# A matrix product by Strassen's scheme on one core: the first product of six regions in quarters, its sums on VectorE, kept sums of b for two more column pairs, and output stored in pairs of row tiles

## The chip, the core and the metric

The kernel runs on one core of a Trainium2 chip. A core has five engines that run side by side and meet through semaphores: TensorE (matmuls; called PE in the profile, its weight loads PEld), VectorE (DVE), ScalarE (ACT), GpSimd (POOL) and SyncE (SP). TensorE writes to PSUM, which has 8 banks of 512 float32 columns by 128 partitions; the other data lie in SBUF, and DMA queues move them from and to DRAM. A queue belongs to the engine that issues into it. Here SP issues plain copies, ScalarE a few, and POOL the loads that round float32 to float16 on the way. Every engine runs its instructions in the order in which the program lists them.

The metric is device time in microseconds (us) of one execution, the median of several.

## What is computed

```
a, b: 4096 x 4096, float32, normally distributed;  alpha = 0.01
x = a @ b
out = where(x > 0, x, alpha * x)
```

## The kernel before

**Regions.** The output is cut into 4 groups g of 1024 rows and 4 pairs j of two 512-column tiles. One (g, j) is a region of 1024 x 1024 results, four blocks of 512 x 512. Region (0, 0) is made plainly at the start. The other 15 follow in the order of a list: (0, 1) to (0, 3); then (1, 2), (1, 0), (1, 3), (1, 1); (2, 2), (2, 0), (2, 3), (2, 1); and (3, 2), (3, 0), (3, 1), (3, 3). The last region of groups 0 to 2 is called turning: the next group's rows of a are brought in and transposed there.

**Seven products.** Each region is a 2 x 2 block product, with the inner dimension of 4096 cut in two halves of 2048, by Winograd's form of Strassen's scheme: seven products of 512 x 2048 by 2048 x 512 in place of eight. A half of the inner dimension consists of two tiles k of 1024 rows. The products are numbered from 0: a11·B11, a12·B21, s2·T2, s3·T3, s1·T5, a22·T4 and s4·B22, where s1 to s4 are sums of blocks of a, made once for a group, and the T are sums of blocks of b, made by VectorE for every region, in place, by `b_sum` (L603) on tiles of 128 x 4096: T3 = B22 - B12 in B12's tile, T2 = B11 + T3 in B11's, T4 = B21 - T2 in B21's, T5 = B22 - T2 in B11's tile again. The order in a region is product 0, then T3 and T2, product 1, T4, product 2, T5, product 4, product 3, product 5, product 6. The program's names call the last four fifth, fourth, sixth and seventh.

**Plain and in quarters.** A plain product (`product`, L831) has 64 matmuls of 512 columns: 2 tiles k, 8 chunks of 128 rows, 4 row tiles mt, each mt with a bank of its own. A product in quarters applies the scheme once more to one product: seven quarter products (`quarter_product`, L770) of 16 matmuls with 256 columns, each with sums of quarters of its operands, of 2048 elements a partition (`sums_of_b` L702 to L706, `t3_of_b` L696). Quarter sums of a's operands s1, a22 and s4 are made once for a group (`sums_of_a`, L719, in the group's second region for s1) and stored in DRAM; later regions load them (`load_sums`, L762). Quarter sums of s3 are made by `sums_of_s3` (L753). In groups 1 to 3, in the regions that are neither the first of their group nor turning, products 4, 3, 5 and 6 are in quarters; 0, 1 and 2 are plain. The set `FIFTH` names the regions with product 4 in quarters: they are just those seven.

**Banks.** Four banks hold y, four hold z. Product 0 goes to y; ScalarE copies y to z (L1132); product 1 adds to z, which is copied out (`keep`, L844) as block u1; product 2 adds to y, and so on. y and z change places from region to region. The leaky step (`leaky`, L313) runs on VectorE, and `leave` stores a block: one DMA of 256 KB for every row tile of 128 rows, on SP (L1076).

**Rooms.** Three rooms of a pool called a16 hold quarter sums, squares and loaded pieces in turn: a new tile waits for the last use of the one whose room it takes. A larger pool x holds the s tiles and a tile q of four quarter sums. s2 is loaded anew for every region, one half k by `load_s2` at the end of the region before, the other during T3: a small memset on VectorE (L788) stands ahead of that load (L789).

**Loads of b.** `fetch_b` and `fetch_unit` load the next region's blocks as soon as a tile is free: from b by POOL with rounding (L547), or, where a float16 copy was kept in DRAM, by SP (L542, L544). For the pair j = 2 (`CACHED`) the sums T3 and T2 are kept too, by group 1, and groups 2 and 3 load them (`move_t`, L529): T3 in place of B12, T2 on ScalarE's queue once product 0 has read B11.

**Measures.** The kernel judges whether its inputs are regular enough for this scheme: `Measure` squares four pieces of a block on ScalarE (L231; three in `begin`, one in `end`) and folds them on VectorE (L240 to L264). `EARLY` and `MEASURED` name the blocks that a region measures. The first entry of `EARLY` begins ahead of product 0 and ends behind it; a second one begins after the copies to z and ends after T2; the entry `middle` (B22 in (3, 0) and (3, 3)) likewise.

## Time and profile before

| what | value |
|---|---|
| median of 3 runs | 1524.78 us (1524.66 to 1526.13) |
| the profiled execution's own time | 1526.13 us |
| its span, first to last instruction | 1524.2 us |
| granted TensorE clock | 0.999 of full speed |
| regions (1, 0), (1, 3) | 91.85 and 91.90 us |
| regions (2, 0), (2, 3), (3, 0), (3, 1) | 90.34, 90.35, 90.34 and 90.35 us |
| DMA traffic | 372.29 MB, 244 GB/s on average |

A row of a timeline gives the start in us from the span's start, the length, the engine, the line of the kernel, the operation, the tile written and those read, shapes, and how many equal instructions were merged. In square brackets is the engine's idle time before it and what ended that. A matmul's length overlaps with the next one's start, so rates are read from start to start. "DMA to landing" is the time from issue to the last byte. The chain of waits is followed back from the last instruction: at each step to what released it.

### The profile page before, as it was taken

How to read it: one execution, taken by the hardware profiler on the slowest of the kernel's cores; microseconds unless marked ns; L12 is line 12 of the kernel's file. 1: busy time of each engine (PE TensorE's matmuls, PEld its weight loads, DVE VectorE, ACT ScalarE, POOL GpSimd, SP SyncE). 2: the span in 40 equal slices, each digit the busy share in tenths (PEclk: the TensorE clock that was granted, in tenths of full speed). 3: DMA queues.
4: the chain of work that ended last, by engine and by line, in shares of the span. 5: the costliest groups of instructions: out<-in, count | busy, mean ns of one | idle time of the engine just before them, and what ended most of it. 6: DMA issues, size and time to landing. Idle time of an engine off the chain costs nothing.

```text
span 1524.2 us, 22803 instructions
## 1 busy us (share of the span) xinstructions
PE 1512.9 (99%) x9003; PEld 879.2 (58%) x9003; DVE 1166.7 (77%) x1221; ACT 512.2 (34%) x885; POOL 258.3 (17%) x426
## 2 busy tenths in 40 slices
PE   9999999999999999999999999999999999999998
PEld 4444444444446577584544748667554475848667
DVE  4588867666896597777779598777978779888797
ACT  2411535537410123124661132323574113252221
POOL 5641110233202011012320101000331100101000
PEclk9999999999999999999999999999999999999999
DMA  9999995999889999999898968859999894968935
GB/s 247 189 215 206 242 285 164 174 187 193 235 330 247 285 300 288 290 289 271 199 273 317 287 252 187 312 151 330 220 239 313 223 337 148 276 238 205 331 122 172
DMA packets 197767, 372.29 MB, mean 244 GB/s; under 512 B 19345, under 2 KB 132241, under 8 KB 184594
## 3 DMA queue, kind: packets, MB, share of 16 engines
q0 software_dynamic: 119808, 112.22, 46.7%
q1 hardware_dynamic: 71218, 232.95, 41.0%
q10 hardware_dynamic: 6624, 25.56, 4.3%
q8 instruction: 72, 1.18, 0.3%
q14 instruction: 45, 0.37, 0.1%
HBM read 359.66 MB, written 121.11 MB: 315 GB/s over the span
## 4 chain that ended last, share of the span: by engine, by line
PE 58%; DMA 6%; DVE 1%; issue 1%; SPq 0%; POOL 0%; DVEq 0%; POOLq 0%
PE ps L831 34%; PE ps L770 25%; DMA b<-in_b_dram 5%; DMA q<-kept_qs 1%; DVE b L603 0%; DVE c L313 0%; DVE c L1028 0%; POOL b L547 0%; SPq L1076 0%; DVE b L696 0%; DVE b L1225 0%; SPq L762 0%; DVEq L603 0%; DVEq L313 0%; POOLq L547 0%
## 5 line engine op out<-in xcount | busy, mean ns | idle before, releaser
L831 PE MATMUL ps<-b,a 128*128 128x512 f16 x2624 | 570.6, 379 | 0.0
L831 PEld LDWEIGHTS <-a 128*128 128x128 f16 x2624 | 256.7, 98 | 307.8
L831 PE MATMUL ps<-b,s 128*128 128x512 f16 x1792 | 391.3, 379 | 0.0
L831 PEld LDWEIGHTS <-s 128*128 128x128 f16 x1792 | 175.4, 98 | 210.9
L603 DVE TENSOR_TENSOR b<-b 128x4096 f16<-128x4096 f16 x97 | 218.9, 2286 | 51.3 <-DMA b<-in_b_dram 33.1
L547 POOL DMA_DIRECT2D b<-in_b_dram x128 | 94.8, 745 | 870.5 <-PE ps L770 266.1
L770 PEld LDWEIGHTS <-q 128*128 128x128 f16 x1872 | 182.6, 98 | 23.2 <-DMA q<-kept_qs 1.6
L844 ACT COPY c<-ps 128x512 f32<-128x512 f32 x164 | 85.9, 596 | 287.5 <-PE ps L831 277.7
L133 POOL DMA_DIRECT2D a<-in_a_dram x252 | 137.5, 553 | 246.5 <-ACT junk L622 81.3
L142 DVE STREAM_TRANSPOSE a<-a 128x512 uint32<-128x512 uint32 (+2 forms) x120 | 127.0, 1107 | 66.5 <-DMA a<-in_a_dram 66.5
L313 DVE SCALAR_TENSOR_TENSOR c<-c 128x1024 f32<-128x1024 f32 (+2 forms) x123 | 141.9, 1196 | 17.7 <-ACT c L844 17.4
L622 ACT ACTIVATE junk<-a 128x512 bf16<-128x512 f16 x192 | 121.2, 631 | 72.8 <-DMA a<-in_a_dram 67.7
L770 PEld LDWEIGHTS <-a 128*128 128x128 f16 x1200 | 117.4, 98 | 14.7
L231 ACT ACTIVATE sq<-b 128x2048 bf16<-128x2048 f16 x60 | 111.3, 1911 | 43.1 <-DVE sq L240 36.7
L770 PE MATMUL ps<-b,q 128*128 128x256 f16 x1008 | 118.6, 273 | 0.0
L283 PE MATMUL ps<-b,a 128*128 128x512 f16 x512 | 112.2, 379 | 0.5 <-ACT a L380 0.2
L770 PEld LDWEIGHTS <-s 128*128 128x128 f16 x960 | 93.8, 98 | 14.2 <-DVE b L603 1.3
L770 PE MATMUL ps<-q,q 128*128 128x256 f16 x864 | 99.9, 273 | 0.9 <-DMA q<-kept_qs 0.9
L770 PE MATMUL ps<-b,a 128*128 128x256 f16 x752 | 88.3, 273 | 0.0
L283 PEld LDWEIGHTS <-a 128*128 128x128 f16 x512 | 49.7, 98 | 60.8 <-issue 1.4
L1132 ACT COPY ps<-ps 128x512 f32<-128x512 f32 x60 | 32.8, 572 | 147.8 <-PE ps L831 147.8
L1063 DVE TENSOR_TENSOR c<-ps,c 128x512 f32<-128x512 f32 x72 | 44.6, 683 | 47.6 <-PE ps L831 38.0
(125 smaller groups left out, 1053.6 us busy)
## 6 DMA issues: line engine op xcount, KB each, us to landing
b<-in_b_dram POOLq DMA_DIRECT2D x136, 512.0 KB, 12.4
out_dram<-c SPq DMA_DIRECT2D x240, 256.0 KB, 7.8
a<-in_a_dram POOLq DMA_DIRECT2D x244, 128.0 KB, 5.7
b<-kept_half SPq DMA_DIRECT2D x28, 1024.0 KB, 11.8
b<-kept SPq DMA_DIRECT2D x20, 1024.0 KB, 9.2
q<-kept_qs ACTq DMA_DIRECT2D x40, 512.0 KB, 7.2
s<-kept_s SPq DMA_DIRECT2D x18, 1024.0 KB, 9.1
q<-kept_qs SPq DMA_DIRECT2D x28, 512.0 KB, 6.1
```

Source lines behind the costliest of these rows:

```text
L133: nc.gpsimd.dma_start(a16[32 * q:32 * q + 32], src.rearrange("(g i) w -> i g w", i=32))
L142: nc.vector.transpose(part.rearrange("p c m e -> p c (m e)").bitcast(U32) .rearrange("p c (g i) -> p g c i", i=32), src[:, :, i * n:(i + 1 ...
L231: nc.scalar.activation(to, self.parts[n], SQUARE)
L283: nc.tensor.matmul(ps, a_cols(at[0, h, u], c, mt, (h, u) == (0, 0)), bt[0, u, nt][:, c, :], start=first, stop=last,)
L313: nc.vector.scalar_tensor_tensor(t, t, alpha, t, op0=MULT, op1=MAX if alpha <= 1 else MIN)
L547: nc.gpsimd.dma_start(t[:, c:c + 4, :], b_rows(j, u, c, 4, nt, g > 0))
L603: nc.vector.tensor_tensor(f(to), f(x0), f(x1), op)
L622: nc.scalar.activation(junk, piece[:, q, :], SQUARE, accum_out=to[:, 4 * n + q:4 * n + q + 1])
L770: nc.tensor.matmul(to[m], xq[:, c // 2, rows, c % 2], yq[:, c, :], start=first and c == 0 and m < banks, stop=c == KC - 1, skip_group_chec ...
L831: nc.tensor.matmul(banks[mt], a_cols(t, c, mt, t is first_a), B(half, nt, k)[:, c, :], start=first and (k, c) == todo[0], stop=(k, c) == t ...
L844: nc.scalar.copy(kept[mt], banks[mt])
L1063: nc.vector.tensor_add(to, bank, to)
```

## The change

Line numbers of the changed kernel are 6 to 117 higher than before for the same statement.

1. A set `FIRST` of six regions replaces `FIFTH`: (1, 0), (1, 3), (2, 3), (3, 0), (3, 1) and (3, 3). The region (2, 0) is not in it. In these product 0 is in quarters (`first_in_quarters`). The sums of quarters of a11 and of B11 are made by VectorE (`for_the_first`), in pieces between the quarter products of the seventh product of the region before, into rooms that that product gives free. The last sum of b is made inside product 0.
2. In these six regions a bank holds a quarter of a block (two row tiles by 256 columns) rather than a row tile of 512 columns, so products 1 and 2 have 128 matmuls of 256 columns each. Adds and copies go by quarters. The banks are dealt out anew: y and z rotate so that product 0 finds free banks, and its first copy goes to the bank that the seventh product called "other".
3. In these regions all entries of `EARLY` begin after product 0's copies and end after T2, and the first half of s2 is loaded after product 0. `EARLY` itself is dealt out differently: (2, 0) has none, (1, 1) measures B11, (3, 0) measures B21, (3, 1) only B21.
4. T3 and T2 of the pairs 0 and 3 are stored in group 2 and loaded in group 3. Where T2 is loaded, a measure begins and ends at once, and the memset and load of s2's second half come behind it.
5. `leave` stores two row tiles by one DMA of 512 KB.

```diff
+KEPT_T = {CACHED: 1, 0: 2, 3: 2}
...
+    def places(g, h, mt, j, nt):
+        row = ((g * 2 + h) * MT + mt) * P
+        col = (j * 2 + nt) * NT
+        return out[row:row + 2 * P, col:col + NT].rearrange("(m p) n -> p m n", p=P)
...
-        if g > 1 and j == CACHED and (half, nt) == (0, 1):
-            move_t("t3", t, u, False)
+        if g > KEPT_T.get(j, G) and (half, nt) == (0, 1):
+            move_t("t3", j, t, u, False)
...
-        (1, 3): [B11], (2, 0): [B21], (2, 3): [B21], (2, 1): [B12], (3, 1): [B11, B21],
+        (1, 3): [B11], (1, 1): [B11], (2, 3): [B21], (2, 1): [B12], (3, 0): [B21], (3, 1): [B21],
...
-    FIFTH = {(1, 0), (1, 3), (2, 0), (2, 3), (3, 0), (3, 1), (3, 3)}
+    FIRST = {(1, 0), (1, 3), (2, 3), (3, 0), (3, 1), (3, 3)}
...
-        ybank = 0 if i % 2 == 0 else 4
-        zbank = 4 - ybank
+        in_first = (g, j) in FIRST
+        if in_first:
+            shared_bank = Z[1]
+            Y, Z = [Z[2], Z[3], Y[0], Z[0]], [Y[1], Y[2], Z[1], Y[3]]
+        else:
+            Y, Z = Z, Y
...
         def product(n, banks, first):
             name, half, nt = PRODUCTS[n]
+            if in_first:
+                for k in ks:
+                    for q in (0, 1, 3, 2):
+                        for c in range(KC):
+                            for m, to in enumerate(into(banks[q])):
+                                nc.tensor.matmul(
+                                    to, a_cols(operand(g, name, k), c, q // 2 * 2 + m),
+                                    B(half, nt, k)[:, c, q % 2 * HALF:(q % 2 + 1) * HALF],
+                                    start=False, stop=(k, c) == (ks[-1], KC - 1), skip_group_check=True,
+                                )
+                return
...
+        def for_the_first(tq, sq, first_t, first_s):
+            y1 = quarters_of_b(i + 1, 0, 0)
+            x1 = {key: by_chunk(q) for key, q in quarters_of_a(g, "a11").items()}
...
+            first_s[1] = new_a16()
+            tt(fx(1), x1[1, 0], x1[1, 1], ADD)
+            yield
+            first_s[2] = tq[4]
+            tt(fx(2), fx(1), x1[0, 0], SUB)
+            yield
+            first_t[3], first_t[2] = new_a16(), tq[2]
+            tt(f(3), y1[1, 1], y1[0, 1], SUB)
+            tt(f(2), f(3), y1[0, 0], ADD)
+            yield
+            first_t[1], first_s[3] = new_a16(), tq[1]
+            tt(f(1), y1[1, 1], f(2), SUB)
+            tt(fx(3), x1[0, 0], x1[1, 0], SUB)
+            yield
+            first_s[4] = sq[3]
+            tt(fx(4), x1[0, 1], fx(2), SUB)
+            yield
+
+        def first_in_quarters(y, shared, z, tq, sq):
...
+            one, other, third, chain = y
...
+            quarter_product(x[0, 0], b[0, 0], into(chain), True)
+            nc.scalar.copy(one, chain)
+            quarter_product(sx(1), t(1), into(shared), True)
+            nc.scalar.copy(room, pair(shared))
+            tq[4] = new_a16()
+            nc.vector.tensor_tensor(t(4), b[1, 0], t(2), SUB)
+            quarter_product(sx(2), t(2), into(chain))
+            nc.scalar.copy(other, chain)
+            quarter_product(x[0, 1], b[1, 0], into(one))
+            nc.scalar.copy(z[0], one)
+            quarter_product(sx(3), t(3), into(chain))
+            nc.scalar.copy(third, chain)
+            nc.vector.tensor_add(pair(chain), pair(chain), room)
+            quarter_product(sx(4), b[1, 1], into(other))
+            nc.vector.tensor_add(pair(other), pair(other), room)
+            quarter_product(x[1, 1], t(4), into(third))
+            z[2] = new_bank(Z[2])
+            for to, bank in ((3, chain), (1, other), (2, third)):
+                nc.scalar.copy(z[to], bank)
...
-                for m in range(2):
-                    nc.sync.dma_start(place(g, h, 2 * r + m, j, nt), t[:, m, :])
+                nc.sync.dma_start(places(g, h, 2 * r, j, nt), t)
...
+        have_t2 = g > KEPT_T.get(j, G)
+        at_once, afterwards = ([], early) if in_first or have_t2 else (early[:1], early[1:])
+        for m in at_once:
             m.begin()
...
+        if in_first:
+            shared = new_bank(shared_bank)
+            first_in_quarters(y, shared, z, first_t, first_s)
+            new_s(g, "s2")
+            load_s2(g, ks[0])
+        else:
+            product(0, y, True)
...
+        for m in afterwards:
+            m.begin()
+            if have_t2:
+                m.end()
...
         for k in ks:
             if have_t2:
+                if late_s2:
+                    load_s2(g, ks[1], True)
                 break
...
-            if g == 1 and j == CACHED:
-                move_t("t3", B(0, 1, k), k, True)
-                move_t("t2", B(0, 0, k), k, True)
+            if g == KEPT_T.get(j):
+                move_t("t3", j, B(0, 1, k), k, True)
+                move_t("t2", j, B(0, 0, k), k, True)
         if middle:
             middle.end()
-        for m in early[1:]:
+        for m in [] if have_t2 else afterwards:
             m.end()
...
-                kept_c = seventh_in_quarters(*rest)
+                first_t, first_s = {}, {}
+                between = for_the_first(tq, sq, first_t, first_s) if next_first else nothing()
+                kept_c = seventh_in_quarters(*rest, between)
                 fetch_b(i + 1, [(1, 1)], (1, 0))
-                new_s(g, "s2")
-                load_s2(g, 1)
+                if not next_first:
+                    new_s(g, "s2")
+                    load_s2(g, 1)
```

In the built program VectorE's instructions of the changed kernel follow each other so, from the end of product 0 in (1, 3) (rows 324 to 345 of the order; line, operation, tiles, size):

```
324 L319 TensorScalarPtr c<-c 128x1024 x2
325 L1105 TensorTensor q_4863<-b,q 128x2048
326 L1112 TensorTensor ps<-ps,c 128x512
327 L1114 TensorTensor ps<-ps,c 128x512
328 L610 TensorTensor b<-b 128x4096
329 L795 Memset s_4954 128x1
330 L610 TensorTensor b<-b 128x4096 x3
331 L246 TensorTensor sq<-sq 128x2048
...
338 L270 TensorTensor stats<-stats,r 128x16 x3
339 L319 TensorScalarPtr c<-c 128x1024 x2
340 L610 TensorTensor b<-b 128x4096 x3
341 L703 TensorTensor b<-b 128x8x256
342 L1342 TensorTensor b<-b 128x8x256 x2
```

And in (3, 0):

```
674 L319 TensorScalarPtr c<-c 128x1024 x2
675 L1105 TensorTensor q_10871<-b,q 128x2048
676 L1112 TensorTensor ps<-ps,c 128x512
677 L1114 TensorTensor ps<-ps,c 128x512
678 L760 TensorTensor s_10200<-a_9977,a_9784 128x4x512
679 L726 TensorTensor q_10965<-s_9869 128x2048
...
682 L726 TensorTensor q_10974<-s_9869,q_10968 128x2048
683 L246 TensorTensor sq<-sq 128x2048
...
690 L270 TensorTensor stats<-stats,r 128x16 x3
691 L795 Memset s_10962 128x1
692 L246 TensorTensor sq<-sq 128x2048
...
699 L270 TensorTensor stats<-stats,r 128x16 x3
700 L319 TensorScalarPtr c<-c 128x1024 x2
701 L610 TensorTensor b<-b 128x4096 x3
```

More of the change, by code (lines that the diff above doesn't have):

```diff
@@ L800 @@
     in_quarters = False
+    Y, Z = [4, 5, 6, 7], [0, 1, 2, 3]
     for i, (g, j) in enumerate(regions):
@@ L839, in new_c, with onto, pieces, add_pieces @@
             return pairs, [pairs[mt // 2][:, mt % 2, :] for mt in range(MT)]
+        def onto(y, r, n):
+            if in_first:
+                return into(y[2 * r + n])
+            return [y[2 * r + m][:, n * HALF:(n + 1) * HALF] for m in range(2)]
+        def pieces(pairs, banks):
+            if in_first:
+                return [(pairs[q // 2][:, :, q % 2 * HALF:(q % 2 + 1) * HALF], pair(banks[q])) for q in range(4)]
+            return [(pairs[mt // 2][:, mt % 2, :], banks[mt]) for mt in range(MT)]
         def keep(banks, side):
             pairs, kept = new_c(side)
-            for mt in range(MT):
-                nc.scalar.copy(kept[mt], banks[mt])
+            for to, bank in pieces(pairs, banks):
+                nc.scalar.copy(to, bank)
             return pairs, kept
+        def add_pieces(pairs, banks):
+            for to, bank in pieces(pairs, banks):
+                nc.vector.tensor_add(to, bank, to)
         def fourth_in_quarters(banks, tq, sx):
@@ L933, in fifth_in_quarters @@
             last = copied(1, 1, chain)
+            if in_first:
+                more(1, 0, last)
+                more(1, 1, last)
+                return
             for m in range(2):
@@ L986, in sixth_in_quarters, with seventh_in_quarters @@
             return next_t, next_s
-        def seventh_in_quarters(y, one, other, tq, sq):
+        def seventh_in_quarters(y, one, other, tq, sq, between):
             pairs, kept = new_c(side)
@@ L1118 @@
         in_fourth = in_quarters and not first_of_group
-        in_fifth = (g, j) in FIFTH
+        next_first = not final and regions[i + 1] in FIRST
         second_of_group = in_fourth and regions[i - 2][0] != g
         early = [measure(i, *block) for block in EARLY.get((g, j), [])]
-        for m in early[:1]:
+        have_t2 = g > KEPT_T.get(j, G)
+        at_once, afterwards = ([], early) if in_first or have_t2 else (early[:1], early[1:])
+        for m in at_once:
             m.begin()
@@ L1228 @@
                 t3_of_b(y7)
-                if not in_fifth:
-                    tq = {n: new_a16() for n in (2, 1)}
-                    sums_of_b(y7, tq, (2, 1))
         if late_ones:
```

158 lines of the change are left out of this document (82 added, 76 removed).

## The prediction

> **What bounds the kernel now.** I read the page first, then TensorE's timeline, then VectorE's, ScalarE's and the DMA's rows in the regions that the change touches.
>
> ```profile
> span 1524.2 us, 22803 instructions
> PE 1512.9 (99%) x9003; PEld 879.2 (58%) x9003; DVE 1166.7 (77%) x1221; ACT 512.2 (34%) x885; POOL 258.3 (17%) x426
> ```
>
> TensorE is busy for 1512.9 of 1524.2 us. Time falls only where matmul time goes away and nothing new makes TensorE wait. Its timeline from the seventh product of (2,0) through (2,3) (start, length, engine, line, operation, tiles):
>
> ```profile
> 954.71 3.66 PE L770 MATMUL ps<-b,s 128*128 128x256 f16 x32
> ...
> 966.93 27.79 PE L831 MATMUL ps<-b,a 128*128 128x512 f16 x128
> 994.56 13.98 PE L831 MATMUL ps<-b,s 128*128 128x512 f16 x64
> 1008.37 3.66 PE L770 MATMUL ps<-b,s 128*128 128x256 f16 x32
> ```
>
> From start to start, 64 matmuls of 512 columns take 1008.37 - 994.56 = 13.81 us (215.8 ns each), and the 112 of 256 columns of a product in quarters 966.93 - 954.71 = 12.22 us (109.1 ns each; one quarter product 1.75 us). Products 0, 1 and 2 of (2,3) follow each other without a wait, 41.44 us together.
>
> **Part 1: the matmuls.** Product 0 in quarters saves 13.81 - 12.22 = 1.59 us. But in the six regions products 1 and 2 also become 256 columns wide, so that they fit the new banks: 128 x 109.1 ns = 13.96 us each, 0.15 more. Net 1.59 - 0.30 = 1.29 us a region, 7.7 us for six, if TensorE never waits.
>
> There are 112 + 256 = 368 weight loads in place of 192, and the page has their length:
>
> ```profile
> L770 PEld LDWEIGHTS <-q 128*128 128x128 f16 x1872 | 182.6, 98 | 23.2 <-DMA q<-kept_qs 1.6
> ```
>
> 98 ns lie under a matmul of 109.1 ns, as in the 112 above, so I take 0 for them; rival (d) prices the other case. The Trainium skill, "TensorE: Matmul & The Clock Gate", section "Back-to-back issue gap", speaks against the change: loads and matmuls together set the pace there, at about 131 ns for 512 columns and 81 for 128. Interpolated (an estimate: 98 ns for 256 columns), product 0 would cost 112 x 98 - 64 x 131 ns = 2.6 us more and products 1 and 2 4.2 each, 66 us in six regions. The trace disagrees: 215.8 ns for 512 columns.
>
> **Part 2: a new wait at the third quarter product.** The sums for product 0 are made in the seventh product of the region before, interleaved by hand, and VectorE runs them in program order. Each waits for the quarter product that last reads the room it takes. The sum from T(3) on stands behind the fifth quarter product of the seventh (8.73 us after that product's start), and seven VectorE operations follow: sums 3, 2, 1 of b, sum 3 of a, one add of a bank into the output, sum 4 of a, and a second add of the bank called "other". The first copy of product 0 writes that bank, so it waits for the second add, and the third quarter product waits for the copy. VectorE's prices, and a ScalarE copy of a bank:
>
> ```profile
> 965.44 0.69 DVE L1005 TENSOR_TENSOR c<-ps,c 128x512 f32<-128x512 f32 x1 [5.74 <-issue]
> 967.75 0.69 DVE L1009 TENSOR_TENSOR c<-ps,c 128x512 f32<-128x512 f32 x1 [1.61 <-ACT c L1008]
> 968.36 2.47 DVE L1011 TENSOR_TENSOR c<-ps,c 128x512 f32<-128x512 f32 x4
> ...
> 1012.23 1.23 DVE L702 TENSOR_TENSOR q<-b 128x2048 f16<-128x2048 f16 x1
> 1013.49 1.22 DVE L704 TENSOR_TENSOR q<-b,q 128x2048 f16<-128x2048 f16 x1
> 1014.63 1.22 DVE L706 TENSOR_TENSOR q<-b,q 128x2048 f16<-128x2048 f16 x1
> ```
>
> ```profile
> 947.92 0.57 ACT L965 COPY ps<-ps 128x512 f32<-128x512 f32 x1 [2.87 <-PE ps L770]
> ```
>
> A sum of 2048 elements takes 1.26 us to the next one if that reads it, 1.14 if not; an add of a bank takes 0.61 to the next. From 8.73 + 0.25 (the row at 965.44 starts so long after the sixth quarter product, 954.71 + 6 x 1.747 = 965.19): 1.26 + 1.26 + 1.14 + 1.14 + 0.61 + 1.14 + 0.69 = 7.24, so the second add ends at 16.2 us and the copy at 16.85. TensorE wants the third quarter product at 12.22 + 2 x 1.75 = 15.7. It waits 1.1 us, between 0 (if the adds run ahead) and 2 us. That leaves 0.2 us of the 1.29.
>
> After that VectorE has four adds (2.4 us), two leaky passes (2.3) and the sum for the last quarter product: 16.2 + 2.4 + 2.3 + 1.2 = 22.1 us against 23.9 when TensorE needs it. No further wait there. The two adds inside PSUM and the copies of ScalarE lie beside quarter products of 1.75 us.
>
> **Part 3: (2,3), (3,1), (3,3).** The measure now runs after product 0. In us from the region's start: the last add ends at 1.1 + 10.48 + 0.25 + 0.6 = 12.4, four big sums of 2.3 (the rows at 618.70 and 623.77 below) at 21.6, the measure's fold of 7.1 (priced in part 4) at 28.7, leaky passes 31, three big sums and a half one 39, against product 2's end at 13.3 + 27.9 = 41.2: 2 us are over. In (3,3) the four sums fall away, and judging takes their place. Each region keeps 0.2 us: -0.6 us.
>
> **Part 4: (1,3), where data come late.** VectorE's timeline, TensorE's, and a row of the chain that ended last:
>
> ```profile
> 618.70 2.29 DVE L603 TENSOR_TENSOR b<-b 128x4096 f16<-128x4096 f16 x1 [9.37 <-DMA b<-in_b_dram]
> ...
> 623.77 4.68 DVE L603 TENSOR_TENSOR b<-b 128x4096 f16<-128x4096 f16 x2 [0.40 <-DMA b<-in_b_dram]
> 628.36 2.35 DVE L313 SCALAR_TENSOR_TENSOR c<-c 128x1024 f32<-128x1024 f32 x2
> ...
> 642.02 1.22 DVE L702 TENSOR_TENSOR q<-b 128x2048 f16<-128x2048 f16 x1
> ```
>
> ```profile
> 637.50 1.91 PE L770 MATMUL ps<-b,s 128*128 128x256 f16 x16
> ...
> 644.28 1.92 PE L770 MATMUL ps<-q,q 128*128 128x256 f16 x16 [0.87 <-DMA q<-kept_qs]
> ```
>
> ```profile
> 632.97 11.27 DMA q<-kept_qs
> ```
>
> and SP's issues of the u1 stores, ahead of it:
>
> ```profile
> 629.61 2.54 SPq L1076 DMA_DIRECT2D out_dram<-c  x4
> ```
>
> T3 and T2 wait 9.37 and 0.40 us for B22, whose loads are released by the region before, and from 618.70 VectorE works without a pause up to product 4 (the fifth). The measure of B11 lay before 618.70, in that idle time. In the changed program its fold stands between T2 and the leaky pass (rows 331 to 338 of the order, L246 to L270), so all that follows 628.36 moves by a measure's length. In (3,0) that length is seen: 1277.45 - 1270.35 = 7.10 us (rows below). Sum 2 of product 4's quarters, done at 642.02 + 1.22 = 643.24, is then done at 650.35; the piece of s1, issued behind the leaky pass and two stores, at about 632.97 + 7.1 - 1.2 + 11.27 = 650.1 (two of four issues fall away, 2.54 / 2). TensorE starts the fourth quarter product at 650.4 instead of 644.28: +6.1 us, product 0's saving included. Bounds: +3 if B22 comes 3 us earlier, +8 if the s1 pieces land 2 us later.
>
> **Part 5: (3,0), two measures behind each other.** VectorE, ScalarE, TensorE:
>
> ```profile
> 1251.99 1.23 DVE L753 TENSOR_TENSOR s<-a,a 128x2048 f16<-128x2048 f16 x1
> ...
> 1260.09 1.23 DVE L719 TENSOR_TENSOR q<-s,q 128x2048 f16<-128x2048 f16 x1 [3.35 <-DMA kept_qs<-q]
> ...
> 1270.35 1.22 DVE L240 TENSOR_TENSOR sq<-sq 128x2048 bf16<-128x2048 bf16 x1
> ...
> 1273.54 1.23 DVE L243 TENSOR_TENSOR sq<-sq 128x2048 bf16<-128x2048 bf16 x1 [0.65 <-ACT sq L231]
> ...
> 1277.45 2.35 DVE L313 SCALAR_TENSOR_TENSOR c<-c 128x1024 f32<-128x1024 f32 x2
> ...
> 1291.20 1.23 DVE L702 TENSOR_TENSOR q<-b 128x2048 f16<-128x2048 f16 x1
> ```
>
> ```profile
> 1261.35 5.51 ACT L231 ACTIVATE sq<-b 128x2048 bf16<-128x2048 f16 x3 [0.59 <-DVE q L719]
> 1271.60 1.91 ACT L231 ACTIVATE sq<-b 128x2048 bf16<-128x2048 f16 x1 [4.74 <-DVE sq L240]
> ```
>
> ```profile
> 1245.91 27.79 PE L831 MATMUL ps<-b,a 128*128 128x512 f16 x128
> 1273.53 13.98 PE L831 MATMUL ps<-b,s 128*128 128x512 f16 x64
> ...
> 1292.59 1.91 PE L770 MATMUL ps<-q,q 128*128 128x256 f16 x16
> ```
>
> In the changed order the sum at 1251.99 stands behind the add that follows the sixth quarter product of product 0: product 0 starts at 1245.91, plus the wait 1.1, six quarters 10.48, 0.25 and an add 0.6, so 1258.35. The last sum of s1 comes 8.10 us later as before (it waits for a store), at 1266.45, and ends at 1267.7. The squares of B21 need rooms that these sums and stores free: four of them, 4 x 1.84, to 1275.1. From L243 on, 3.91 us to the end of the fold: 1279.0. The squares of B22 need rooms from the first measure's L243 (1276.4), stand behind its squares on ScalarE, and end at 1283.8; then 3.91 us: the leaky pass starts at 1287.7, not 1277.45, though the four big sums (9.1 us) are gone. Everything to the fourth quarter product of product 4 is VectorE's order: sum 2 ended at 1292.43 with 0.16 us to spare, and now ends at 1302.7. +10.1 us.
>
> Also on that queue stands the memset (L788) that releases the load of s2's second half, now behind the first fold:
>
> ```profile
> DMA to landing us min/median/max: 4.7/9.1/17.8
> ```
>
> Issued at 1279.1, landed at 1284 to 1288 (median), while TensorE wants it at 1245.91 + 13.3 + 13.96 + 6.98 = 1280.2: product 2 waits, but ends by 1295, before the sums. It decides nothing unless it takes over 10 us. The upper bound of part 5 is from the slower stores in (1,0):
>
> ```profile
> 510.30 1.22 DVE L753 TENSOR_TENSOR s<-a,a 128x2048 f16<-128x2048 f16 x1
> ...
> 521.15 1.22 DVE L719 TENSOR_TENSOR q<-s,q 128x2048 f16<-128x2048 f16 x1 [6.10 <-DMA kept_qs<-q]
> 526.40 2.29 DVE L603 TENSOR_TENSOR b<-b 128x4096 f16<-128x4096 f16 x1 [4.03 <-DMA b<-in_b_dram]
> ...
> 532.83 4.62 DVE L603 TENSOR_TENSOR b<-b 128x4096 f16<-128x4096 f16 x2 [1.40 <-DMA b<-in_b_dram]
> ```
>
> There the same step takes 10.85 us, 2.75 more, and twice (the squares wait for the last store too): +15.6. The lower bound is +7, if the squares find rooms at once.
>
> **Part 6: (1,0).** The chain is DMA-gated: the sum at 510.30 moves by 6.4 us as in (3,0), to 516.7, the last sum of s1 to 516.7 + 10.85 = 527.5 and its end to 528.7; the T3 at 526.40 follows there, and two sums of 2.3 later the T3 at 532.83 starts at 533.3. So (1,0) keeps nothing of its 1.29 and loses 0.4 us.
>
> **Part 7: what lies beside.** T3 and T2 of pairs 0 and 3 are written in (2,0) and (2,3), four stores of 1 MB on SP behind the sums, ahead of the u1 stores and the s1 pieces; in (3,0) and (3,3) T3 comes by SP instead of POOL's loads and T2 by ScalarE's queue, issued when product 0 ends and wanted when product 1 does, 13.96 us later. The same move in the second pair lands in
>
> ```profile
> DMA to landing us min/median/max: 5.8/10.0/12.3
> ```
>
> so I take 0, at worst 2 us in each. Paired stores halve SP's issues and move the same bytes: 0, beyond the 1.2 us used in part 4. In (1,1) the measure of B11 runs during product 0, beside 27 us of products: 0.
>
> **The sum.** +0.4 (1,0), +6.1 (1,3), -0.2 (2,3), +10.1 (3,0), -0.4 for (3,1) and (3,3): +16.0. Durations come from an execution of 1526.13 us (span 1524.2), the longest of the three runs; on it, 1542.1 us. Against the median of 1524.78, 1.35 lower, I predict 1541 us.
>
> **The rivals.** (a) VectorE's queue is not last at product 4. For it: VectorE is busy 77% of the span, and eight new sums and two adds, 8 x 1.14 + 2 x 0.61 = 10.3 us in a region of 90, would fit. Against it: its rows from 618.70 and 1260.09 on show no pause before TensorE's waits. It decides if the fold in (1,3) ends before T3 starts (618.70) and that in (3,0) before 1270; then all six regions keep up to 1.29 us: 1524.8 - 7.7 = 1517. Chance 0.07. (b) One of the two places pays only: B22 lands early in (1,3), or rooms are free in (3,0): 1531 to 1535. Chance 0.15. (c) The stores in (3,0) take what they took in (1,0), and the T2 loads are late too: 1541 + 5.5 + 2 = 1548.5. Chance 0.12. (d) The weight loads of the narrow matmuls do not stay hidden: every tenth open is 36.8 x 98 ns = 3.6 us a region, 22 us in six on top of 1541: 1563. For it: 109.1 - 98 leaves 11 ns. Against it: 112 in a row lose nothing. Chance 0.01. (e) Savings and waits cancel within 0.2% (about 3 us, what this kernel's measurement can tell from no change): 0.03. The forecast has 0.62.
>
> **How the numbers follow.** (b), the forecast (1537 to 1547 by parts 4 and 5) and (c) cover 1531 to 1550. Faster 0.07, same 0.03, slower 0.90.
>
> **What would show it.** Right: L1101's copy released by VectorE and about 1.1 us of wait in the third quarter product of product 0; in (1,3) the fold between T2 and the leaky pass and a wait of some 7 us ahead of product 4; in (3,0) the leaky pass at 28 us and more after product 1's start, product 2 broken by the load of s2, and product 4 some 10 us late. Wrong: TensorE without gaps from product 0 to product 4 in either region, or gaps released by loads of b and T2 instead of VectorE.

## The result, and the profile after the change

| | before | after |
|---|---|---|
| median | 1524.78 us | 1550.77 us (1546.98 to 1551.11, five runs) |
| the profiled execution's own time | 1526.13 us | 1546.98 us |
| its span | 1524.2 us | 1545.2 us |

After to before the ratio is 1.0162, with a 95% interval of 1.0148 to 1.0176. That is 24.7 us of 1524.78; by the two medians it is 26.0 us. The prediction was 1541 us with a range of 1531 to 1550; the median lies 0.8 us above the range's upper end, and 1524.78 us times the ratio, 1549.5, just inside it. The two profiled executions differ by 20.85 us only, because that of before was 1.35 us above its median and that of after, the fastest of its five, 3.79 below (1.35 + 3.79 + 20.85 = 25.99). So regions are compared by the two profiles, and totals by the ratios. The ratios of the experiments below are to runs of the kernel before on the same chip, whose medians were 1525.6 to 1526.4 us there.

The head of the page of the changed kernel:

```profile
span 1545.2 us, 24785 instructions
PE 1510.3 (98%) x10059; PEld 984.3 (64%) x10059; DVE 1211.4 (78%) x1249; ACT 525.9 (34%) x909; POOL 252.3 (16%) x418
```

TensorE is busy for 1510.3 us, 2.6 less than before, while the span is 21.0 longer. The time went into waits, and the view that adds up TensorE's waits (engine, line, what it waited for; us in total, times, longest) names them:

```profile
PE ps L777 <- DVE b L610: 9.6, 2, 6.2
PE ps L835 <- DMA s<-kept_s: 7.7, 1, 7.7
PE ps L777 <- ACT ps L1101: 6.4, 6, 1.2
PE ps L835 <- DVE b L610: 1.5, 1, 1.5
...
PE ps L777 <- DMA q<-kept_qs: 1.0, 1, 1.0
```

Lines are those of the changed kernel: L610 is `b_sum`, L1101 the first copy of product 0, L777 a quarter product, L835 a matmul of products 1 and 2. A region's time is read on TensorE's timeline, from the start of its product 0 to that of the next region:

| region | before | after | difference | predicted |
|---|---|---|---|---|
| (1, 0) | 91.85 | 93.73 | +1.88 | +0.4 |
| (1, 3) | 91.90 | 97.94 | +6.04 | +6.1 |
| (2, 3) | 90.35 | 90.27 | -0.08 | -0.2 |
| (3, 0) | 90.34 | 104.58 | +14.24 | +10.1 |
| (3, 1) | 90.35 | 90.27 | -0.08 | -0.2 |
| (3, 3), to its last quarter product | 88.71 | 88.63 | -0.08 | -0.2 |

All others agree within 0.02 us. The six rows make 21.92 us. The spans differ by 21.0 because the stretch from the last quarter product's start to the end is 1.2 us shorter (7.72 for 8.93), and the regions of group 0 together 0.2 us longer.

**The new wait in every region of `FIRST`.** VectorE's, ScalarE's and TensorE's timelines in (3, 0), whose product 0 starts at 1253.98:

```profile
1256.28 1.22 DVE L1088 TENSOR_TENSOR q<-a,q 128x2048 f16<-128x2048 f16 x1
1257.41 0.69 DVE L1057 TENSOR_TENSOR c<-ps,c 128x512 f32<-128x512 f32 x1
```

```profile
1258.18 0.57 ACT L1101 COPY ps<-ps 128x512 f32<-128x512 f32 x1 [2.92 <-DVE c L1057]
```

```profile
1258.80 1.91 PE L777 MATMUL ps<-q 128*128 128x256 f16 x16 [1.16 <-ACT ps L1101]
...
979.77 1.91 PE L777 MATMUL ps<-q 128*128 128x256 f16 x16 [1.03 <-ACT ps L1101]
```

The add of L1057 ends at 1258.1, the copy runs from 1258.18, and the third quarter product waits 1.16 us for it. The second matmul row is the same place in (2, 3).

**(1, 3).** VectorE and TensorE:

```profile
620.18 2.29 DVE L610 TENSOR_TENSOR b<-b 128x4096 f16<-128x4096 f16 x1 [9.44 <-DMA b<-in_b_dram]
...
629.66 1.22 DVE L246 TENSOR_TENSOR sq<-sq 128x2048 bf16<-128x2048 bf16 x1
...
636.88 2.35 DVE L319 SCALAR_TENSOR_TENSOR c<-c 128x1024 f32<-128x1024 f32 x2
```

```profile
625.56 14.14 PE L835 MATMUL ps<-b,s 128*128 128x256 f16 x128
645.90 4.96 PE L777 MATMUL ps<-b,s 128*128 128x256 f16 x32 [6.20 <-DVE b L610]
...
652.45 1.91 PE L777 MATMUL ps<-q,q 128*128 128x256 f16 x16
```

T3 still starts when B22's load has landed. From the fold's first instruction to the leaky pass (L319) there are 636.88 - 629.66 = 7.22 us, and TensorE waits 6.20 us ahead of product 4. Its first 32 matmuls then take 4.96 us in place of 3.66; the last section comes back to that.

**(3, 0).** VectorE, ScalarE and TensorE:

```profile
1266.60 1.22 DVE L760 TENSOR_TENSOR s<-a,a 128x2048 f16<-128x2048 f16 x1
...
1278.58 1.23 DVE L726 TENSOR_TENSOR q<-s,q 128x2048 f16<-128x2048 f16 x1 [7.24 <-DMA kept_qs<-q]
...
1291.29 0.06 DVE L795 MEMSET s<- 128x1 f16 x1
...
1299.86 2.36 DVE L319 SCALAR_TENSOR_TENSOR c<-c 128x1024 f32<-128x1024 f32 x2
```

```profile
1280.01 7.32 ACT L237 ACTIVATE sq<-b 128x2048 bf16<-128x2048 f16 x4 [11.65 <-DMA kept_qs<-q]
1288.61 7.31 ACT L237 ACTIVATE sq<-b 128x2048 bf16<-128x2048 f16 x4 [1.29 <-DVE sq L249]
```

```profile
1281.51 7.15 PE L835 MATMUL ps<-b,s 128*128 128x256 f16 x64
1296.33 9.19 PE L835 MATMUL ps<-b,s 128*128 128x256 f16 x64 [7.67 <-DMA s<-kept_s]
1308.88 1.92 PE L777 MATMUL ps<-b,s 128*128 128x256 f16 x16 [3.37 <-DVE b L610]
```

The chain is as forecast: product 0's adds, the sums of s1, the squares of one block, the memset that lets s2's second half be loaded, the squares of the other block, the leaky pass. But one link is longer: the last sum of s1 waits 7.24 us for a store, against 3.35 before, and the leaky pass starts 45.88 us after the region's start, where 41.8 had been forecast.

### The profile page after: what moved, and what is told of

Its sections match the earlier page's. It is cut to its first block, busy times and chain, and to the rows that moved or that the text cites. A ratio compares the mean times of both kernels' runs of the same rounds, so it can differ in the third digit from the quotient of the medians.

```text
span 1545.2 us, 24785 instructions
## 1 busy us (share of the span) xinstructions
PE 1510.3 (98%) x10059; PEld 984.3 (64%) x10059; DVE 1211.4 (78%) x1249; ACT 525.9 (34%) x909; POOL 252.3 (16%) x418
## 4 chain that ended last, share of the span: by engine, by line
PE 87%; DVE 5%; DMA 4%; issue 2%; ACT 2%; SPq 0%; DVEq 0%; POOL 0%; ACTq 0%
PE ps L854 46%; PE ps L777 29%; PE ps L289 7%; PE ps L835 5%; ACT sq L237 1%; DMA kept_qs<-q 1%; DMA b<-in_b_dram 1%; DMA q<-kept_qs 1%; DVE c L319 1%; DVE b L610 1%; DMA s<-kept_s 0%; DVE q L1081 0%; DVE q L1080 0%; DVE q L1085 0%; DVE q L1088 0%
## 5 line engine op out<-in xcount | busy, mean ns | idle before, releaser
L854 PE MATMUL ps<-b,a 128*128 128x512 f16 x1856 | 403.9, 379 | 0.0
L854 PEld LDWEIGHTS <-a 128*128 128x128 f16 x1856 | 181.6, 98 | 218.3
L854 PE MATMUL ps<-b,s 128*128 128x512 f16 x1408 | 307.5, 379 | 0.0
L854 PEld LDWEIGHTS <-s 128*128 128x128 f16 x1408 | 137.8, 98 | 165.7
L777 PEld LDWEIGHTS <-q 128*128 128x128 f16 x2256 | 220.3, 98 | 34.8 <-issue 7.8
L610 DVE TENSOR_TENSOR b<-b 128x4096 f16<-128x4096 f16 x89 | 200.8, 2286 | 33.7 <-DMA b<-in_b_dram 27.8
L777 PEld LDWEIGHTS <-a 128*128 128x128 f16 x1488 | 145.6, 98 | 17.9
L319 DVE SCALAR_TENSOR_TENSOR c<-c 128x1024 f32<-128x1024 f32 (+2 forms) x123 | 142.1, 1196 | 13.0 <-ACT c L877 12.7
L777 PE MATMUL ps<-b,q 128*128 128x256 f16 x1104 | 130.0, 273 | 1.0 <-DMA q<-kept_qs 1.0
L777 PE MATMUL ps<-q,q 128*128 128x256 f16 x1056 | 122.8, 273 | 0.1
L289 PE MATMUL ps<-b,a 128*128 128x512 f16 x512 | 112.2, 379 | 0.5 <-ACT a L386 0.2
L777 PE MATMUL ps<-b,a 128*128 128x256 f16 x944 | 111.2, 273 | 0.0
L777 PEld LDWEIGHTS <-s 128*128 128x128 f16 x960 | 94.4, 99 | 23.0 <-DVE b L610 10.1
L835 PE MATMUL ps<-b,s 128*128 128x256 f16 x768 | 87.0, 276 | 9.2 <-DMA s<-kept_s 7.7
L289 PEld LDWEIGHTS <-a 128*128 128x128 f16 x512 | 49.7, 98 | 60.8 <-issue 1.4
L835 PEld LDWEIGHTS <-s 128*128 128x128 f16 x768 | 76.0, 99 | 19.4 <-DVE sq L248 7.9
## 6 DMA issues: line engine op xcount, KB each, us to landing
b<-kept_half SPq DMA_DIRECT2D x28, 1024.0 KB, 12.3
```

The costliest lines, as they stand in the source:

```text
L289: nc.tensor.matmul(ps, a_cols(at[0, h, u], c, mt, (h, u) == (0, 0)), bt[0, u, nt][:, c, :], start=first, stop=last,)
L319: nc.vector.scalar_tensor_tensor(t, t, alpha, t, op0=MULT, op1=MAX if alpha <= 1 else MIN)
L610: nc.vector.tensor_tensor(f(to), f(x0), f(x1), op)
L777: nc.tensor.matmul(to[m], xq[:, c // 2, rows, c % 2], yq[:, c, :], start=first and c == 0 and m < banks, stop=c == KC - 1, skip_group_chec ...
L835: nc.tensor.matmul(to, a_cols(operand(g, name, k), c, q // 2 * 2 + m), B(half, nt, k)[:, c, q % 2 * HALF:(q % 2 + 1) * HALF], start=False, ...
L854: nc.tensor.matmul(banks[mt], a_cols(t, c, mt, t is first_a), B(half, nt, k)[:, c, :], start=first and (k, c) == todo[0], stop=(k, c) == t ...
```

## The experiments

The theory was that VectorE's order sets the loss at three places: the add ahead of product 0's first copy, the fold in (1, 3), and two measures behind the sums of s1 in (3, 0). The main rival was that loads and stores do it.

**1. The sums made later.** Sums 3 and 4 of a11 are wanted by the fifth and sixth quarter products only, so they can stand behind the second add.

```diff
             tt(f(1), y1[1, 1], f(2), SUB)
-            tt(fx(3), x1[0, 0], x1[1, 0], SUB)
             yield
+            yield
+            tt(fx(3), x1[0, 0], x1[1, 0], SUB)
             first_s[4] = sq[3]
             tt(fx(4), x1[0, 1], fx(2), SUB)
...
             nc.vector.tensor_add(block(1, 1), pair(other), block(1, 1))
+            next(between)
             add_pieces(pairs, y)
```

> The changed kernel, with the sums 3 and 4 of a11's quarters moved behind the second add of the bank called other. Theory (VectorE's order holds that add, the add holds the first copy of product 0, the copy holds TensorE): the wait of 1.03 to 1.16 us ahead of the third quarter product is gone in all six regions. (2, 3), (3, 1) and (3, 3) keep all of it: 90.27 us becomes about 89.2 each. In (1, 0) and (3, 0) the sums of s1 come 1.1 us earlier, so 1.1 us less each. In (1, 3) nothing, since B22's loads set the time there. Together 5.3 us less than the changed kernel: about 1545. Rival (the copy waits for its bank in some other way, or ScalarE is late): the waits stay and the time with them, 1550.

Measured: 1544.68 us, ratio 1.0130 (1.0113 to 1.0147). No wait stands at L1101 any more, and TensorE's timeline in (2, 3) shows product 0 without a gap:

```profile
975.01 1.91 PE L777 MATMUL ps<-b,a 128*128 128x256 f16 x16
976.76 1.91 PE L777 MATMUL ps<-q,q 128*128 128x256 f16 x16
978.51 1.91 PE L777 MATMUL ps<-q 128*128 128x256 f16 x16
```

(2, 3) and (3, 1) take 89.08 us, (3, 3) 87.43: 1.27 to 1.28 less than before the change. (1, 0) gains 0.66 and not 1.1. (3, 0) gains nothing (105.06): its sums of s1 start earlier but wait 7.22 us for a store again, and product 2 waits 8.52 us for s2. So in (2, 3), (3, 1) and (3, 3) the order of seven VectorE operations was the whole reason that product 0 in quarters kept nothing; what (3, 0) waits for is not VectorE alone.

**2. B21's measure back in (2, 0).**

```diff
-        (1, 3): [B11], (1, 1): [B11], (2, 3): [B21], (2, 1): [B12], (3, 0): [B21], (3, 1): [B21],
+        (1, 3): [B11], (1, 1): [B11], (2, 0): [B21], (2, 3): [B21], (2, 1): [B12], (3, 1): [B21],
```

> The changed kernel, with the measure of B21 of pair 0 in (2, 0), as in the kernel before, in place of (3, 0). Theory (two measures stand one behind the other ahead of the leaky pass and of the load of s2): the leaky pass of (3, 0) starts 8.5 us earlier (37.4 us after the region's start, not 45.9), the wait of 7.67 us for the second half of s2 in product 2 falls under 1 us, and (3, 0) takes about 96 us in place of 104.6; (2, 0) stays at 90.35. In all 8.5 us less than the changed kernel, about 1542. What stays, 6 us over before, is the sums of s1 that stand behind product 0's adds, and TensorE waits about 5 us ahead of product 4. Rival (T3 and T2 loaded late by SP and ScalarE): (3, 0) stays over 100.

Measured: 1541.87 us, ratio 1.0106 (1.0089 to 1.0123). (2, 0) stays at 90.34; (3, 0) falls to 97.99, the wait for s2 is gone, and the leaky pass starts at 37.7 us. One measure behind the other costs 6.6 us of the 14.24. Product 4 waits 5.04 us as expected; 2 us more than expected are in the slower matmuls behind that wait (6.04 us for 32 in place of 3.66):

```profile
1302.37 6.04 PE L777 MATMUL ps<-b,s 128*128 128x256 f16 x32 [5.04 <-DVE b L610]
```

**3. The fold ahead of T3 in (1, 3).**

```diff
             m.begin()
-            if have_t2:
+            if have_t2 or g == 1:
                 m.end()
...
-        for m in [] if have_t2 else afterwards:
+        for m in [] if have_t2 or g == 1 else afterwards:
```

> The changed kernel, with the measure of B11 in (1, 3) ended ahead of T3 and T2 instead of behind them. Theory (the fold stands between T2 and the leaky pass, where VectorE is on the path; ahead of T3 it waits for B22's loads anyway): the fold ends at about 623.8, 3.6 us after T3 started in the changed kernel, T3 and T2 move by that, product 2 waits some 3 us for T2 of the first half, the wait of 6.2 us ahead of product 4 falls under 3 us, the granted clock no longer falls to a half there, and (1, 3) takes 92.9 to 93.5 us in place of 97.9: about 4.5 us less in all, 1546. Rival (the loads of B22 and of the pieces of s1 set the time alone): (1, 3) stays at 97 to 98 us.

Measured: 1546.10 us, ratio 1.0130 (1.0113 to 1.0147). (1, 3) and (1, 1) together take 189.78 us in place of 193.05 (187.01 before the change): 3.3 us gained, where 4.5 had been expected. T3 starts at 623.69, product 2 waits 2.58 us for T2, and nothing waits ahead of product 4. But product 2 itself takes 15.80 us in place of 14.14, at a lower clock after a short wait, where none had been expected:

```profile
628.35 15.80 PE L835 MATMUL ps<-b,s 128*128 128x256 f16 x128 [2.58 <-DVE b L610]
```

**4. B11's measure left out in (1, 3).**

```diff
-        (1, 3): [B11], (1, 1): [B11], (2, 3): [B21], (2, 1): [B12], (3, 0): [B21], (3, 1): [B21],
+        (1, 1): [B11], (2, 3): [B21], (2, 1): [B12], (3, 0): [B21], (3, 1): [B21],
```

> The changed kernel without the measure of B11 in (1, 3), which is left out altogether (the kernel then judges its inputs without that block). Theory (the fold between T2 and the leaky pass is the whole loss there): the leaky pass starts 7.2 us earlier, at 629.7, TensorE no longer waits for T5 ahead of product 4, its clock stays, and (1, 3) with (1, 1) takes 185.6 to 186.9 us in place of 193.05, no more than the 187.01 of before: B22's late loads then set the time. In all 6.2 to 7.4 us less than the changed kernel. Rival (product 0's order or the s1 pieces hold it as well): over 188.5.

Measured: 1542.12 us, ratio 1.0107 (1.0090 to 1.0124). (1, 3) and (1, 1) take 185.63 us, 7.4 less than in the changed kernel and 1.4 less than before. The leaky pass starts at 630.17, and product 4 starts without a wait:

```profile
630.17 2.35 DVE L319 SCALAR_TENSOR_TENSOR c<-c 128x1024 f32<-128x1024 f32 x2
```

```profile
639.90 3.66 PE L777 MATMUL ps<-b,s 128*128 128x256 f16 x32
```

So the measure is the whole loss in (1, 3) (that its fold's place matters, experiment 3 shows); product 0 in quarters, with the wait at L1101 still in it, loses nothing there. Whether it gains is not shown: the five kernels below with a plain product 0 in (1, 3) take 186.1 to 187.3 us for the two regions.

**5. Product 0 plain everywhere.**

```diff
-    FIRST = {(1, 0), (1, 3), (2, 3), (3, 0), (3, 1), (3, 3)}
+    FIRST = set()
```

> The changed kernel with FIRST empty: product 0 plain in all regions; kept T3 and T2, paired stores and the new places of the measures stay. Theory (product 0 in quarters, with its order on VectorE, makes most of the loss): (1, 0) and (1, 3) are back at 91.9 us, (2, 3), (3, 1) and (3, 3) at 90.35; in (3, 0) two measures still stand one behind the other, but the sums of s1 start 6.5 us earlier, so that the leaky pass comes at 35.4 us after the region's start against 31.5 before: 94.0 us. The end is about 1 us shorter than before by the paired stores, as in the changed kernel. In all 1524.8 + 3.7 - 1.1 = 1527.4. Rival (the transfers of the kept T and the paired stores make the loss): over 1535.

Measured: 1533.54 us (1531.94 to 1535.36), ratio 1.0053 (1.0037 to 1.0070), six us more than expected. (1, 3) with (1, 1) takes 186.10 us and (1, 0) 92.54; (2, 3), (3, 1) and (3, 3) are as before. All that is lost is lost in (3, 0): 100.06 us, not 94.0. So with a plain product 0 as well the rest of the change costs 9.7 us there. ScalarE's timeline in (3, 0) shows what had been overlooked:

```profile
1259.72 0.33 ACTq L536 DMA_DIRECT2D b<-kept_t  x1
...
1260.16 0.37 ACTq L536 DMA_DIRECT2D b<-kept_t  x1
1260.63 3.71 ACT L237 ACTIVATE sq<-b 128x2048 bf16<-128x2048 f16 x2 [0.15 <-issue]
1270.13 3.71 ACT L237 ACTIVATE sq<-b 128x2048 bf16<-128x2048 f16 x2 [5.79 <-DMA kept_qs<-q]
```

Two squares run; the third waits 5.79 us for its room, until the store of the last sum of s1 has landed. That store was issued at 1260.37, just behind the two loads of T2 (1 MB each), and took 9.68 us; before the change it took 2.65. A new theory: the loads of T2 hold up the stores of s1, and the squares wait for the stores.

**6. No loads of T2 in (3, 0).**

```diff
             for k in ks:
+                if j == 0:
+                    break
                 t = have_b[i, k, 0] = b_pool.tile([P, KC, NT], DT, name="b", tag="b11")
                 move_t("t2", j, t, k, False, nc.scalar)
```

> The changed kernel without the loads of T2 in (3, 0): the products that read T2 there read B11, so the results of that region are not the reference's. Theory (new, from the run with product 0 plain: the two loads of 1 MB on ScalarE's queue run beside the stores of the sums of s1, which take 9.7 us in place of 5.6, and the sums' last one and the squares wait for rooms that those stores free): the stores take about 5.6 us again, the last sum of s1 waits 3.4 us in place of 7.24, the first square starts 4 us earlier, the leaky pass at about 41.5 us after the region's start in place of 45.9, and (3, 0) takes 99 to 100.5 us in place of 104.6. In all 4 to 5.5 us less than the changed kernel. Rival (the stores are slow for another reason, or the order on VectorE and ScalarE alone sets the time): (3, 0) stays at 104 to 106.

Measured: 1545.91 us, ratio 1.0122 (1.0107 to 1.0138); (3, 0) takes 100.32 us, 4.26 less than in the changed kernel. Experiments 3 and 4, which leave (3, 0) alone, have 106.21 and 105.64 us there, so the region scatters by up to 1.6 us, and 100.32 lies below all of these. The DMA view of 1255 to 1285 us (transfer, queue, count, KB each, median us to landing), first of the changed kernel, then of this one:

```profile
b<-kept_t ACTq DMA_DIRECT2D x2, 1024.0 KB, 9.0
kept_qs<-q SPq DMA_DIRECT2D x4, 512.0 KB, 9.5
```

```profile
kept_qs<-q SPq DMA_DIRECT2D x4, 512.0 KB, 4.4
```

and VectorE's last sum of s1 here:

```profile
1275.43 1.22 DVE L726 TENSOR_TENSOR q<-s,q 128x2048 f16<-128x2048 f16 x1 [2.19 <-DMA kept_qs<-q]
```

The stores take 4.4 us in place of 9.5, and the sum waits 2.19 us in place of 7.24. T2 itself was on time in the changed kernel (issued from 1267.89 on, landed by 1278.87, and product 1 ended after 1281). Its loads cost some 4.3 us all the same, through the stores beside them.

**7. (3, 0) with product 0 in quarters and nothing else new in it.** This is kernel 9 (below) with one region more.

```diff
-    FIRST = {(2, 3), (3, 1), (3, 3)}
+    FIRST = {(2, 3), (3, 0), (3, 1), (3, 3)}
```

> As three_k3, with (3, 0) also in FIRST: its product 0 in quarters, T3 and T2 made there, one measure, no loads of T2. Theory (the sums of s1 stand behind product 0's adds on VectorE, 5.3 us later than with product 0 plain, and all that follows to product 4 is VectorE's order): the last sum of s1 starts about 19.5 us after the region's start (17.4 in three_k3 less its earlier start, 14.6 in the kernel before), the leaky pass at 36.9 in place of 31.5, and (3, 0) takes 95 to 96.5 us in place of 90.35: 1527, slower than the kernel before. Rival (only the two measures and the slow stores cost, the place of the sums of s1 does not): 89.1 us in (3, 0), 1520.7.

Measured: 1526.26 us, ratio 0.9999 (0.9990 to 1.0009). (3, 0) takes 94.22 us against 90.35 in kernel 9. (The bracket in the expectation is a slip: in kernel 9, as in the kernel before, the last sum of s1 starts 14.2 us after the region's start; here it does at 17.4.) The stores were faster than assumed, so the leaky pass starts at 34.7 us and not 36.9, and product 4 waits 3.38 us. With s1's sums behind product 0's adds and nothing else new, the region loses 3.9 us, 1.6 of them in slow matmuls after the wait. The mechanism of the prediction's part 5 holds.

**8 and 9. Only what pays.** `FIRST` = (2, 3), (3, 1), (3, 3), with edits 1 and 2; kernel 9 also keeps no T of pair 0.

```diff
-KEPT_T = {CACHED: 1, 0: 2, 3: 2}
+KEPT_T = {CACHED: 1, 3: 2}
...
-    FIRST = {(1, 0), (1, 3), (2, 3), (3, 0), (3, 1), (3, 3)}
+    FIRST = {(2, 3), (3, 1), (3, 3)}
```

> The changed kernel with FIRST = (2, 3), (3, 1), (3, 3), the sums 3 and 4 of a11's quarters behind the second add, and the measure of B21 of pair 0 in (2, 0); kept T of pairs 0 and 3 and paired stores stay. Theory: the three regions keep 1.2 to 1.3 us each (89.08, 89.08 and 87.43 us, -3.8 together), (1, 0) and (1, 3) stand as in the kernel before, and (3, 0), with one measure that waits for the slow stores, loses 0.5 us. The end 0 to 1 us shorter by the paired stores. 1525.5 - 3.8 + 0.5 - 0.5 = 1521.7, ratio 0.9975: faster than both kernels. Rival (the loads of T2 keep (3, 0) over 94): 1525 or more.

> As three_first, with T3 and T2 of pair 0 not kept, so that (3, 0) is made as in the kernel before. Theory: (3, 0) is back at 90.34 us, the stores of the sums of s1 at 5.6 us; 0.5 us less than three_first, 1521.2, ratio 0.997. Rival (the kept T of pair 0 cost nothing when one measure only stands there): equal to three_first within 0.2 us in (3, 0).

Measured: 1522.64 us, ratio 0.9975 (0.9966 to 0.9984), and 1521.93 us, ratio 0.9972 (0.9961 to 0.9984). Both are faster than the kernel before, by some 4 us. (2, 3), (3, 1) and (3, 3) take 89.08, 89.27 and 87.44 in the first and 89.08, 89.08 and 87.44 in the second. (3, 0) takes 90.34 and 90.35: with one measure and a plain product 0 the loads of T2 cost nothing, though the last store, issued just behind them, still took 8.3 us where kernel 9 has 2.6. The two kernels cannot be told apart by their times.

**10. Paired stores alone**, in the kernel before:

```diff
-                for m in range(2):
-                    nc.sync.dma_start(place(g, h, 2 * r + m, j, nt), t[:, m, :])
+                nc.sync.dma_start(places(g, h, 2 * r, j, nt), t)
```

> The kernel before with its output stored by pairs of row tiles (one DMA of 512 KB for two of 256 KB), and nothing else of the change. Theory (the stores lie beside other work): all regions within 0.2 us of before; after the last matmul the end may be up to 1.8 us shorter, as in the runs with the change (7.1 to 8.8 us from the last quarter product's start, 8.9 before). 1525.5 - 0.5 = 1525.0, ratio 0.9990 to 1.0003. Rival (larger stores hold up the loads of b): some region over 0.5 us longer.

Measured: 1525.48 us, ratio 0.9994 (0.9985 to 1.0003): no difference that can be told. Regions are within 0.1 us of before, but for (1, 3) with (1, 1) (186.30 in place of 187.01). The stretch from the last quarter product's start to the end was 7.7 us here, 8.9 before, 7.7 after the change and 8.8 in kernel 9, so it says nothing on paired stores.

## Why the prediction was right or wrong

**Part 1** (1.29 us a region without waits) was right: 1.27 to 1.28 us, once the wait was out of the way. The rule quoted there from the Trainium skill, that loads and matmuls set the pace at 131 ns for 512 columns, fell with it: the narrow matmuls cost what the rows said. (Another section of the same page of the Trainium skill, "TensorE: Matmul & The Clock Gate", section "Wait — 56ns, not 53.3ns?", gives 215.7 ns for 512 columns, and the trace's 215.8 agrees.) Rival (d) is out.

**Part 2** (a wait of 1.1 us at the third quarter product) was right in place, cause and size: 1.03 to 1.16 us in each of six regions, and gone when two sums were moved.

**Part 3** was right: no further wait in (2, 3), (3, 1) and (3, 3); each kept 0.08 us.

**Part 4** ((1, 3), +6.1) was right: +6.04, and without the measure the loss is gone. The fourth quarter product of product 4 started at 652.45, or 650.34 when the 2.11 us that this region starts later are taken off; forecast was 650.4. The agreement is a little better than the reasoning: 1.3 us of it are matmuls at half clock after the wait, which no term held; VectorE's sum alone, done at 651.8 in this run, would have held TensorE 0.7 us less.

**Part 5** ((3, 0), +10.1) had the chain right and one link too short. The step that failed is "The last sum of s1 comes 8.10 us later as before (it waits for a store)": it came 11.98 us later (1278.58 - 1266.60). Those 3.9 us are nearly the whole miss of 14.24 - 10.1 = 4.1. The bound of +15.6, from the stores in (1, 0), held it, but for another reason than that given. The wait of product 2 for s2 came as described (7.67 us) and decided nothing.

**Part 7** is where that link was lost. Of T2's loads it asked only whether they land before product 1 ends, and took 0, at worst 2 us. They landed in time. (The row it used, 5.8/10.0/12.3 us, is of all twelve moves of L529, stores and loads of T3 among them; the four loads of T2 took 8.7 to 12.3 us.) What it did not ask is what they slow down: the stores of the sums of s1, the first three issued within 3.5 us of the loads, took 9.5 us by the median where they had taken 5.6 in the kernel before,

```profile
kept_qs<-q SPq DMA_DIRECT2D x4, 512.0 KB, 5.6
```

and the last sum and the squares waited for those. That was worth some 4.3 us. For the paired stores and the measure in (1, 1), 0 was right.

**Part 6** ((1, 0), +0.4) was right on VectorE and wrong on TensorE. The last sum of s1 ended at 529.05, which is 528.8 when the 0.23 us of the later start are taken off (forecast 528.7), and the leaky pass moved by 0.4. But these rows of TensorE in the changed kernel show two waits that were not looked for:

```profile
533.63 14.13 PE L835 MATMUL ps<-b,s 128*128 128x256 f16 x128 [1.50 <-DVE b L610]
...
552.74 1.92 PE L777 MATMUL ps<-b,q 128*128 128x256 f16 x16 [0.98 <-DMA q<-kept_qs]
```

Product 2 needs the first half of T2, which VectorE now makes behind the late sums of s1; and a piece of s1 for product 4 lands late. The prediction had followed the chain to the leaky pass only. No run takes these two waits away, so what they cost by themselves is read from the rows alone.

**The rivals.** (a), no wait on VectorE, and (b), one place only, are out: both places cost. (e), savings and waits that cancel, is out too. (c), slow stores in (3, 0) and late loads of T2, was half of what came: slow stores, because of loads that were not late. By the profiles (+20.85, or 1545.6) the outcome lies between the forecast and (c), 1548.5. Against the +16.0 of the sum the regions missed by 4.1 us in (3, 0), 1.5 in (1, 0) and 0.3 in the other four, and the shorter end gave back 1.2; that is luck, since the end took 7.1 to 9.0 us from run to run. What the sum lacked besides is 3.79 us between the profiled execution and the median: four other runs had a mean granted clock of 0.992 to 0.993, the profiled one 0.995, and an estimate from that is 0.0025 x 1548 = 3.9 us. Where in the execution they lie is not shown. A total near the range's edge therefore proves nothing of the parts; the rows above do.

## What to carry to other kernels

When a load is put on another queue, ask not only whether it is in time, but which transfers in flight beside it have somebody waiting: here loads that nobody waited for made stores twice as long, and a chain stood on the stores. When work is inserted into an engine's order by hand, put what is wanted last behind what releases somebody: two sums moved took the wait out of all six regions, and three of them, where nothing else waited, then gained 1.27 us each. And where a region already runs against a late load or a chain of sums, a shorter product there only turns into a longer wait; the change paid in three regions of six.

## What the runs showed of the hardware that was not expected

A wait of TensorE can cost more than its length. The view by stretches (start:end and length in us; busy us and count of PE, PEld, DVE, ACT, POOL; granted clock of TensorE; DMA share; GB/s) of the changed kernel around the wait in (1, 3):

```profile
639.00:641.50 2.50, 0.69 (x7) 0.38 (x4) 2.50 (x3) 1.07 (x2) 0.00 (x0) 1.00 1.02 375
642.00:645.50 3.50, 0.00 (x0) 0.00 (x0) 3.50 (x2) 0.00 (x0) 0.00 (x0) 0.50 1.00 334
646.00:648.50 2.50, 2.50 (x13) 1.76 (x13) 2.50 (x3) 0.00 (x0) 0.00 (x0) 0.50 0.71 292
649.00:652.00 3.00, 3.00 (x30) 2.70 (x28) 2.90 (x4) 0.58 (x1) 0.00 (x0) 1.00 0.00 0
```

The granted clock falls to 0.50 some 2 us into the wait and stays there for 2.7 us after TensorE works again: 13 matmuls in 2.5 us, then 30 in 3.0. Over the runs that cost 1.3 us (4.96 in place of 3.66 for 32 matmuls) to 2.9 us (6.51, behind the same wait of (1, 3) in experiment 2). A short wait is enough at times: without T2's loads TensorE stood from 1290.55 to 1293.15, 2.6 us, and this followed,

```profile
1290.75:1292.50 1.75, 0.00 (x0) 0.00 (x0) 1.22 (x1) 1.75 (x2) 0.00 (x0) 1.00 0.83 351
1293.25:1296.00 2.75, 2.75 (x14) 1.89 (x14) 2.61 (x5) 1.34 (x3) 0.00 (x0) 0.50 0.00 0
```

while the changed kernel's wait of 3.37 us ahead of product 4 in (3, 0) left the clock alone:

```profile
1305.50:1308.50 3.00, 0.01 (x1) 0.00 (x0) 3.00 (x2) 1.07 (x2) 0.00 (x0) 1.00 0.99 313
1309.00:1312.00 3.00, 2.65 (x24) 2.24 (x23) 3.00 (x3) 0.00 (x0) 0.00 (x0) 1.00 0.66 269
```

The Trainium skill, "TensorE: Matmul & The Clock Gate", section "What's actually happening", says that the clock is halved after an idle window of about 3.4 us, and restored after as long a busy one, with windows that run freely. The half and the chance in it agree with these rows; the length of the wait does not, since 2.6 us of standing still sufficed twice (without T2's loads, and in experiment 3). What does come in steps of 3.41 us is the low spell: inside the kernels the granted clock stays at 0.50 for 3.41, 6.83 or once 10.24 us, in the changed kernel from 641.76 to 648.59. Over all twelve traces no wait of TensorE up to 2.4 us brought a low spell and every one of 3.8 us or more did; of seven between, 2.56 to 3.70 us, four did. For a sum of this kind: to a wait of over 2.5 us belongs an allowance of 0 to 3 us for slow matmuls behind it, where TensorE is on the path.
